# Eight of twenty weight subtractions move from GpSimd to VectorE

## The chip, the cores and the metric

The kernel runs on one core of a Trainium2 chip. The time is the device time of one execution in microseconds (us), and lower is better. TensorE multiplies matrices and accumulates in PSUM banks; VectorE, ScalarE and GpSimd do elementwise work; the queue of SyncE (SP) issues the DMAs between device memory and the on-chip SBUF. In the profile they are called PE (with PEld for its weight loads), DVE, ACT, POOL and SP. Each engine takes its own instructions strictly in the order in which they stand in its queue, and waits for the others by semaphores.

## The reference

One layer of a decoder, for 1024 tokens of width 1024, all in float32:

```python
h = rmsnorm(x, norm1_w)
proj = h @ w_in                       # one projection for both mixers
# mixer A: gated DeltaNet, 4 heads of 128; causal conv + silu on q, k, v; z is its gate
o_a = rmsnorm(gated_delta_rule(l2norm(q), l2norm(k), v, g, beta), gdn_norm_w) * silu(z)
# mixer B: dilated sliding-window attention, 8 heads of 64
o_b = dilated_attention(qb, kb, vb)
x = x + concat([o_a, o_b]) @ w_out
h = rmsnorm(x, norm2_w)
u = causal_dwconv(h @ w_up, ffn_conv_w)
x = x + (silu(u[..., :D_FF]) * u[..., D_FF:]) @ w_down
return rmsnorm(x, final_norm_w)
```

The delta rule works on chunks of tokens, and in each chunk a unit lower-triangular system is solved.

## The kernel before

**Products in three parts.** To keep float32 accuracy, each operand of a large product is split into a high part in TensorE's faster format (`whi`, `xhi`) and a low part (`wlo`, `xlo`), the difference between the operand and its high part. A product is then three products, high by high, high by low and low by high (`mm3`, line 200).

**The weights of the input projection.** `dense` (line 496) goes through 29 tiles of weights of 128 by 1024 numbers, in this order by index: 0 is the key tile of DeltaNet head 3; 1 to 8 are the values of the dilated attention; 9 to 16 are the query and value tiles of the four DeltaNet heads, one after the other; 17 to 24 are the query and key tiles of the dilated attention; 25 to 28 are the gate's tiles. The keys of heads 0 to 2 come earlier and are not in this list. While one tile is multiplied, the next is made: a DMA brings the raw weights (`wst`, two buffers), ScalarE copies them to `whi` (two buffers), and another engine subtracts: `wlo = wst - whi` (two buffers). Which engine subtracts is set by `spare` in `weight` (line 217): with it GpSimd, without it VectorE (through `split`, line 208).

**What runs beside it.** TensorE is given its work in an order that a planner (`Weave`) makes from estimated times: the dense products, and between them short products of the chunks. In the stretch that matters here VectorE has four kinds of work in one queue: it scales each half of a finished tile out of its PSUM banks (`xr`, two banks of the tag hf in turn); it adds up the causal convolution (`qT`, `vT`, three instructions each); it scales the attention scores of DeltaNet (`at`, four instructions for each of two banks of the tag atr); and it solves the triangular systems of all heads at once (`forward_sub`: 31 pairs of a product `tmp<-mt,xi` and a subtraction `xi<-xi,tmp`, each of which needs the one before). GpSimd has, beside the subtractions, only small work there: it clears buffers and takes a power for the norm of the queries (`rq<-ssq,mhalf`), which VectorE needs for `gq`.

**Order around the change.** The banks of the tag atr are shared: TensorE turns `qT` into token order there, makes the scores of head after head there, and turns `vT` there. The turns of `vT` (`ps<-ident,vT`, line 197, four to a bank) can start when VectorE has read the scores of the bank before (`at`). When the solve is done, its result goes to device memory and comes back by 24 strided loads on SP's queue (`x<-xdram`, `um<-xtdram`), for small merging products on TensorE. Inside VectorE's queue the order is set when the program is built, by a scheduler that goes by priorities and its own simulated times; what the code writes first need not stand first.

## Time and profile before

| | us |
|---|---|
| median of 3 runs (lowest, highest) | 1204.37 (1203.77, 1204.42) |
| the profiled execution | 1206.67 |
| its span, first to last instruction | 1204.6 |
| TensorE busy | 1191.6 |
| VectorE busy | 916.1 |
| ScalarE busy | 575.3 |
| GpSimd busy | 108.2 |
| subtractions on GpSimd | 20, of 2.38 each (median) |
| subtractions on VectorE, 128x1024 | 16, of 1.22 each (median of its 21) |

The program's instructions stand under the line of the helper that recorded them, so L142 is nearly all of VectorE, ScalarE and GpSimd, and L193 and L197 are TensorE; groups are told apart by their tiles, written out<-in. "Idle before" is the time in which the engine did nothing before an instruction, and what follows the arrow is what ended it. All times in the trace count from the start of the span.

### The profile page before, as it was taken

To read this page: it belongs to the slowest core of one execution; us is meant where nothing else is said; L and a number is where in the kernel's file an instruction comes from. 1 tells how busy PE (TensorE), PEld (TensorE's weight loads), DVE (VectorE), ACT (ScalarE), POOL (GpSimd) and SP (SyncE) were. 2 spreads that over 40 slices of the span, in tenths; PEclk is the share of its full clock that TensorE was granted. 3 is DMA by queue.
4 is the path that set the end of the run, shared out by engine and by line. 5 is a ranking of instruction groups with operands and counts; after the bars stand their busy time and mean duration, and the time that the engine had idled before them with its cause. 6 is when DMAs were issued, how large, how long until landed. Compare 5 with 4: busy or idle time off the path is not lost.

```text
span 1204.6 us, 18326 instructions
## 1 busy us (share of the span) xinstructions
PE 1191.6 (99%) x7068; PEld 987.0 (82%) x7068; DVE 916.1 (76%) x1442; ACT 575.3 (48%) x1126; POOL 108.2 (9%) x98
## 2 busy tenths in 40 slices
PE   9999999999999999999999999999999999999997
PEld 7888778889877778888888888888888888888886
DVE  7583985656365466767989989889898889999875
ACT  7375335456355443655545544444454454444441
POOL 0313232213422110000000000000000000000000
PEclk9999999999999999999999999999999999999998
DMA  7434233435624304444213122131322298547513
GB/s 235 107 93 121 103 109 119 149 115 164 222 94 128 95 36 120 169 140 140 84 56 106 58 100 91 67 105 53 105 73 85 94 370 305 180 162 226 165 54 140
DMA packets 85798, 154.80 MB, mean 129 GB/s; under 512 B 21168, under 2 KB 36304, under 8 KB 85712
## 3 DMA queue, kind: packets, MB, share of 16 engines
q1 hardware_dynamic: 85136, 153.12, 39.1%
q8 instruction: 55, 0.90, 0.3%
q10 hardware_dynamic: 576, 0.52, 0.1%
q14 instruction: 31, 0.25, 0.1%
HBM read 117.68 MB, written 35.93 MB: 128 GB/s over the span
## 4 chain that ended last, share of the span: by engine, by line
PE 93%; DVE 4%; ACT 1%; issue 1%; DMA 1%; SPq 0%; POOLq 0%; POOL 0%; DVEq 0%; ACTq 0%
PE ps L193 43%; PE pa L193 20%; PE dw L193 17%; PE pc L193 10%; PE ps L197 3%; DVE tmp L142 1%; DVE xi L142 1%; PE warm L193 1%; ACT sm L144 0%; DMA mt<-mdram 0%; DVE xr L142 0%; DVE qT L142 0%; DVE vT L142 0%; DMA mdram<-um 0%; DVE x1h L142 0%
## 5 line engine op out<-in xcount | busy, mean ns | idle before, releaser
L193 PE MATMUL dw<-pr 128*128 128x512 f32 (+1 forms) x984 | 211.3, 376 | 0.0
L193 PEld LDWEIGHTS dw<-pr 128*128 128x128 f32 x984 | 176.7, 188 | 33.6
L193 PE MATMUL ps<-xhi,whi 128*128 128x512 f32 x384 | 157.9, 411 | 0.5 <-DVE xr L142 0.5
L193 PE MATMUL ps<-xhi,wlo 128*128 128x512 f32 x384 | 150.5, 392 | 0.0
L193 PE MATMUL ps<-xlo,whi 128*128 128x512 f32 x384 | 150.3, 392 | 0.0
L193 PE MATMUL pa<-T,pair 128*128 128x512 f32 x528 | 127.0, 389 | 0.0
L193 PEld LDWEIGHTS pa<-T,pair 128*128 128x128 f32 x528 | 99.0, 188 | 20.6
L193 PEld LDWEIGHTS ps<-xhi,whi 128*128 128x128 f32 x384 | 72.7, 189 | 19.1 <-issue 5.6
L193 PEld LDWEIGHTS ps<-xhi,wlo 128*128 128x128 f32 x384 | 72.4, 188 | 15.8
L193 PEld LDWEIGHTS ps<-xlo,whi 128*128 128x128 f32 x384 | 72.7, 189 | 12.3
L142 ACT ACTIVATE u<-pa 128x512 f32<-128x512 f32 x44 | 26.3, 598 | 107.3 <-PE pa L193 107.3
L142 ACT ACTIVATE whi<-wst 128x1024 fp32r<-128x1024 f32 (+2 forms) x41 | 41.8, 1019 | 72.1 <-PE ps L193 40.3
L142 DVE SCALAR_TENSOR_TENSOR y<-xu,fcw,y 128x1023 f32<-128x1023 f32 (+1 forms) x44 | 56.4, 1281 | 22.1 <-ACT y L142 22.0
L142 POOL TENSOR_TENSOR rs<-rs,mhalf 128x2 f32<-128x2 f32 (+2 forms) x4 | 4.5, 1116 | 738.7 <-DVE rs L144 738.7
L193 PE MATMUL pc<-T,S 128*128 128x512 f32 x264 | 63.4, 389 | 0.0
L193 PE MATMUL pc<-B,pair 128*128 128x512 f32 x264 | 63.4, 389 | 0.0
L193 PE MATMUL pa<-B,A 128*128 128x512 f32 x264 | 63.4, 389 | 0.0
L193 PE MATMUL pa<-T,S 128*128 128x512 f32 x264 | 63.4, 389 | 0.0
L142 DVE TENSOR_TENSOR wst<-wst 128x512 f32<-128x512 f32 x88 | 60.5, 687 | 0.9
L193 PE MATMUL ps<-B,pair 128*128 128x512 f32 x252 | 60.5, 389 | 0.0
L144 ACT ACTIVATE sm<-sm,mx 128x128 f32<-128x128 f32 (+7 forms) x64 | 35.4, 555 | 47.9 <-DVE mx L144 47.9
L142 POOL TENSOR_TENSOR wlo<-wst,whi 128x1024 fp32r<-128x1024 f32 x20 | 47.9, 2393 | 115.6 <-ACT whi L142 113.7
(246 smaller groups left out, 2417.5 us busy)
## 6 DMA issues: line engine op xcount, KB each, us to landing
wst<-in_wu SPq DMA_DIRECT2D x44, 512.0 KB, 3.7
wd<-in_wd SPq DMA_DIRECT2D x44, 512.0 KB, 4.5
upark<-y SPq DMA_DIRECT2D x22, 512.0 KB, 3.7
wst<-in_wi SPq DMA_DIRECT2D x21, 512.0 KB, 3.7
r<-upark SPq DMA_DIRECT2D x11, 512.0 KB, 7.8
r<-upark SPq DMA_DIRECT2D x22, 256.0 KB, 6.8
wa<-in_wd SPq DMA_DIRECT2D x22, 256.0 KB, 3.1
wst<-in_wv SPq DMA_DIRECT2D x8, 512.0 KB, 3.7
```

What stands on the lines that cost most here:

```text
L142: return getattr(eng, op)(*a, **kw)
L144: return getattr(eng, op)(*a, **kw)
L193: tc.stamp_issue_order_token(nc.tensor.matmul(dst, lhs, rhs, start=start, stop=stop, **kw).ins, TOKEN)
L197: tc.stamp_issue_order_token(nc.tensor.transpose(dst, src, ident if idt is None else idt).ins, TOKEN)
```

## The change

The condition `spare` turns from index 9 on to index 17 on. GpSimd keeps the subtractions of 17 to 28, twelve in all: the query and key tiles of the dilated attention and the gate's four. Those of 9 to 16, the query and value tiles of DeltaNet, go to VectorE.

```diff
@@ -517,7 +517,7 @@
             w = nxt.pop()
             i = place[0] = place[0] + 1
             if i < len(srcs):
-                nxt.append(weight(None, st=raw.pop(), spare=i >= 9))
+                nxt.append(weight(None, st=raw.pop(), spare=i >= 17))
             if i + 1 < len(srcs):
                 raw.append(raw_weight(srcs[i + 1]))
             return w
```

The order of instructions on TensorE and on ScalarE is the same in both programs. Three places of the others follow.

GpSimd loses the eight subtractions; this is the piece of the difference (x_1647 and x_1661 are the buffers that the solve's result comes back to).

```order
 L142 TENSOR_TENSOR nk<-ssk,phalf 128x8 x4
-L142 TENSOR_TENSOR wlo<-wst,whi 128x1024
 L142 MEMSET xi 128x1024
 L142 AFFINE_SELECT xi<-xi 128x1024
-L142 TENSOR_TENSOR wlo<-wst,whi 128x1024 x3
-L142 TENSOR_TENSOR rq<-ssq,mhalf 128x8
-L142 TENSOR_TENSOR wlo<-wst,whi 128x1024 x2
+L142 TENSOR_TENSOR rq<-ssq,mhalf 128x8 x2
 L142 MEMSET x_1647 128x1024
 L142 MEMSET x_1661 128x1024
```

Two of the eight stand ahead of the clearing of `xi` and of the solve, and the others among the solve's steps.

VectorE in the first part of the solve, where the first convolution stands, before:

```order
L142 TENSOR_TENSOR tmp<-mt,xi 128x231
L142 TENSOR_TENSOR xr<-ps,rstdB 128x512
L142 TENSOR_TENSOR xi<-xi,tmp 128x21x11
L142 TENSOR_TENSOR tmp<-mt,xi 128x240
L142 TENSOR_TENSOR xi<-xi,tmp 128x20x12
L142 SCALAR_TENSOR_TENSOR qT<-xr,gcw,qT 128x1023
L142 TENSOR_TENSOR tmp<-mt,xi 128x247
L142 SCALAR_TENSOR_TENSOR qT<-xr,gcw,qT 128x1022
L142 TENSOR_TENSOR xi<-xi,tmp 128x19x13
L142 SCALAR_TENSOR_TENSOR qT<-xr,gcw,qT 128x1021
L142 TENSOR_TENSOR xr<-ps,rstdB 128x512
```

The same place now:

```order
L142 TENSOR_TENSOR xr<-ps,rstdB 128x512
L142 TENSOR_TENSOR tmp<-mt,xi 128x231
L142 TENSOR_TENSOR wlo<-wst,whi 128x1024
L142 TENSOR_TENSOR xi<-xi,tmp 128x21x11
L142 SCALAR_TENSOR_TENSOR qT<-xr,gcw,qT 128x1023
L142 TENSOR_TENSOR tmp<-mt,xi 128x240
L142 SCALAR_TENSOR_TENSOR qT<-xr,gcw,qT 128x1022
L142 TENSOR_TENSOR xi<-xi,tmp 128x20x12
L142 TENSOR_TENSOR xr<-ps,rstdB 128x512
L142 SCALAR_TENSOR_TENSOR qT<-xr,gcw,qT 128x1021
```

One subtraction has come in, the next tile's `xr` stands ahead of the third convolution step, and two steps of the solve (247) have gone behind it.

VectorE at the scores, before:

```order
L142 TENSOR_TENSOR tmp<-mt,xi 128x240
L142 TENSOR_TENSOR xr<-ps,rstdB 128x512
L142 TENSOR_TENSOR xi<-xi,tmp 128x12x20
L142 SCALAR_TENSOR_TENSOR at<-ps,bp,dec 128x128 x4
L142 SCALAR_TENSOR_TENSOR gq<-ngam,rq 128x8
L142 TENSOR_TENSOR tmp<-mt,xi 128x231
L142 TENSOR_TENSOR xi<-xi,tmp 128x11x21
L142 TENSOR_TENSOR tmp<-mt,xi 128x220
L142 SCALAR_TENSOR_TENSOR at<-ps,bp,dec 128x128 x4
```

The same place now:

```order
L142 TENSOR_TENSOR tmp<-mt,xi 128x252
L142 TENSOR_TENSOR xr<-ps,rstdB 128x512
L142 SCALAR_TENSOR_TENSOR at<-ps,bp,dec 128x128 x4
L142 SCALAR_TENSOR_TENSOR gq<-ngam,rq 128x8
L142 TENSOR_TENSOR xi<-xi,tmp 128x14x18
L142 TENSOR_TENSOR tmp<-mt,xi 128x247
L142 SCALAR_TENSOR_TENSOR at<-ps,bp,dec 128x128
L142 TENSOR_TENSOR xi<-xi,tmp 128x13x19
L142 SCALAR_TENSOR_TENSOR at<-ps,bp,dec 128x128 x3
```

The scores stand earlier among the solve's steps: the solve has got to 252 instead of to the subtraction with 12x20 when the first bank is read, which is five steps fewer.

## The prediction

> **What bounds the kernel now.** I read the page first, then TensorE's waits, then the chain of waits around them, then the timelines of the engines there.

> ```profile
> PE 1191.6 (99%) x7068; PEld 987.0 (82%) x7068; DVE 916.1 (76%) x1442; ACT 575.3 (48%) x1126; POOL 108.2 (9%) x98
> PE 93%; DVE 4%; ACT 1%; issue 1%; DMA 1%; SPq 0%; POOLq 0%; POOL 0%; DVEq 0%; ACTq 0%
> ```

> TensorE is busy for 99% of the span and holds 93% of the chain that ended last; VectorE holds 4% of it. TensorE's products are the same and in the same order after the change, so the time moves only by what TensorE waits, or by its clock. The subtractions concerned lie between 110 and 196 us. All of TensorE's waits there that the view of waits names (window 120 to 160) are these three, and none is listed between 160 and 245:

> ```profile
> PE ps L197 <- DVE at L142: 1.6, 1, 1.6
> PE ps L193 <- DVE xr L142: 0.5, 1, 0.5
> PE ps L197 <- DVE gq L142: 0.3, 1, 0.3
> ```

> All three are for VectorE. The chain of waits (window 130 to 160; start, length, what) shows how far back that goes:

> ```profile
> 127.95 2.48 DVE tmp L142
> ...
> 136.15 1.27 DVE qT L142
> ...
> 139.76 0.44 DVE tmp L142
> ...
> 141.70 1.97 DVE xi L142
> ...
> 152.40 1.05 DVE at L142 x4
> 153.49 1.10 PE ps L197 x4
> ```

> For 25 us the chain runs through VectorE's queue, but for one ScalarE step, and it holds two pieces that are far too long: a step of the solve of 2.48 and one of 1.97, beside one of 0.44 between them. The timeline of GpSimd and VectorE (start, length) tells why:

> ```profile
> 127.64 2.53 POOL L142 TENSOR_TENSOR wlo<-wst,whi 128x1024 fp32r<-128x1024 f32 x1 [7.73 <-ACT whi L142]
> 127.95 2.46 DVE L142 TENSOR_TENSOR tmp<-mt,xi 128x220 f32<-128x220 f32 x1
> 130.45 0.39 DVE L142 TENSOR_TENSOR xi<-xi,tmp 128x220 f32<-128x220 f32 x1
> 140.88 2.50 POOL L142 TENSOR_TENSOR wlo<-wst,whi 128x1024 fp32r<-128x1024 f32 x1 [10.71 <-ACT whi L142]
> 141.02 0.68 DVE L142 TENSOR_TENSOR xr<-ps,rstdB 128x512 f32<-128x512 f32 x1
> 141.62 2.04 DVE L142 TENSOR_TENSOR xi<-xi,tmp 128x255 f32<-128x255 f32 x1
> 144.15 0.42 DVE L142 TENSOR_TENSOR xi<-xi,tmp 128x252 f32<-128x252 f32 x1
> ```

> While GpSimd subtracts, a VectorE instruction with two inputs in SBUF does not finish until GpSimd is done; `xr`, with an input in PSUM, runs on. The first held step loses 2.46 - 0.39 = 2.07, the second 2.04 - 0.42 = 1.62. So GpSimd, 9% busy, stands on the chain through VectorE.

> What it costs on TensorE, from its timeline at the three places:

> ```profile
> 137.28 0.39 PE L193 MATMUL ps<-xhi,wlo 128*128 128x512 f32 x1
> 138.17 0.47 PE L193 MATMUL ps<-xhi,whi 128*128 128x512 f32 x1 [0.50 <-DVE xr L142]
> ...
> 139.17 0.39 PE L193 MATMUL ps<-xlo,whi 128*128 128x512 f32 x1
> 139.40 0.39 PE L193 MATMUL ps<-xhi,wlo 128*128 128x512 f32 x1
> 139.91 0.55 PE L197 MATMUL ps<-ident,qT 128*128 128x128 f32 x3
> ```

> ```profile
> 150.62 0.39 PE L193 MATMUL ps<-xhi,wlo 128*128 128x512 f32 x1
> 151.30 0.63 PE L197 MATMUL ps<-ident,vT 128*128 128x128 f32 x4 [0.29 <-DVE gq L142]
> 153.49 1.10 PE L197 MATMUL ps<-ident,vT 128*128 128x128 f32 x4 [1.56 <-DVE at L142]
> 154.24 0.78 PE L193 MATMUL ps<-xhi,whi 128*128 128x512 f32 x1
> ```

> A product takes 0.23 from start to start (139.17 to 139.40). So 137.28 to 138.17 loses 0.66, 139.40 to 139.91 loses 0.28 (the turns wait for ScalarE's `qT`, whose input VectorE finished at 136.15 + 1.27), and 150.62 to 151.30 loses 0.45. Where TensorE stood idle, the loss is the idle time and 0.16, by which a product's row (0.39) otherwise overlaps the next: so the 1.56 ahead of 153.49 are 1.72 lost. Together 3.11. Then the clock, in two windows:

> ```profile
> 150.00:153.54 3.54, 1.69 (x10) 0.98 (x8) 3.47 (x14) 0.05 (x2) 0.71 (x1) 1.00 0.00 0
> 153.54:156.96 3.42, 3.42 (x11) 2.84 (x12) 2.34 (x7) 2.38 (x9) 0.00 (x0) 0.50 0.38 153
> ```

> The columns are window, length, then PE, PEld, DVE, ACT and POOL busy, clock, and DMA. After a stretch with TensorE 1.69 busy of 3.54, it gets half its clock for 3.42 us: 1.71 lost. In all 4.82 us hang on VectorE being late here.

> [...]

> **The change part by part.** Row by row for the subtraction itself (min/median/max in ns, first and last start):

> ```profile
> L142 DVE TENSOR_TENSOR wlo<-wst,whi x21: 558/1224/1227, 4.3 to 540.0; 128x1024 fp32r<-128x1024 f32 x16, 128x768 fp32r<-128x768 f32 x3, 128x384 fp32r<-128x384 f32 x2
> L142 POOL TENSOR_TENSOR wlo<-wst,whi x20: 2352/2382/2532, 110.6 to 452.2; 128x1024 fp32r<-128x1024 f32 x20
> ```

> *GpSimd* loses 8 x 2.38 = 19.1 us. It waited for `whi` before each, so this in itself is worth nothing. *VectorE* gains 8 x 1.22 = 9.8 us. The first two stand ahead of the solve, where VectorE waits anyway:

> ```profile
> 121.56 0.19 DVE L142 TENSOR_TENSOR tmp<-mt,xi 128x31 f32<-128x31 f32 x1 [10.05 <-DMA mt<-mdram]
> ```

> They cost nothing; without that idle time it would be 2.4. The third and fourth stand ahead of the scores: +2.44. Against that the two held steps give back 2.07 + 1.62 = 3.69, and the new order puts five solve steps behind the scores, about 0.41 each as in the rows above: 2.04. VectorE reaches `gq` 3.69 + 2.04 - 2.44 = 3.29 earlier. From `gq` to the end of the second bank it now has two solve steps, one score, one solve step, three scores, 0.12 more than before. It ended those scores at 152.40 + 1.05 = 153.45, and now ends them at 153.45 - 3.29 + 0.12 = 150.28. TensorE, freed of the four stalls, would want that bank at 153.49 - 3.11 = 150.38. So the stall goes with 0.1 to spare: the lead and the need are about equal, and whatever else makes VectorE late comes back on TensorE.

> What else could: VectorE takes over GpSimd's wait for `whi`, and behind it everything in its queue stands.

> ```profile
> 126.50 1.06 ACT L142 ACTIVATE whi<-wst 128x1024 fp32r<-128x1024 f32 x1 [9.06 <-PE ps L193]
> 137.50 1.28 ACT L142 ACT_TABLE_LOAD   x1 [4.44 <-DVE qT L142]
> 139.76 1.04 ACT L142 ACTIVATE whi<-wst 128x1024 fp32r<-128x1024 f32 x1
> 147.78 2.93 POOL L142 TENSOR_TENSOR rq<-ssq,mhalf 128x8 f32<-128x8 f32 x1 [4.40 <-DVE ssq L142]
> ```

> The third `whi` is ready at 127.56, and VectorE gets to its subtraction at about 129.4: no wait. The fourth is ready at 140.80, behind a table load that itself waits for the third step of `qT`. That step comes about 1 earlier now (-2.07, +1.22, +0.6 for `xr`, -0.7 for the two steps gone behind), so `whi` comes at about 139.8, and VectorE gets there at 140.20 - 2.07 + 1.22 + 0.6 = 139.95, where 140.20 is the end of the solve step that stands before it (139.76 + 0.44). No wait then, or 0.9 if ScalarE does not come earlier. I take 0.4, between the ends, since both margins are thin. `rq` (2.93 while VectorE was busy) starts some 3 earlier with its input, and is ready before `gq`.

> The fifth subtraction, too, held a solve step:

> ```profile
> 158.11 2.43 DVE L142 TENSOR_TENSOR xi<-xi,tmp 128x156 f32<-128x156 f32 x1
> ```

> TensorE has no wait from 157 to 245, so what the last four give back is worth nothing, and their 4 x 1.22 = 4.9 in VectorE's queue cost nothing as long as they come back about as they are added. The solve ends later: in the new order the three convolution steps of the second value tile (1.27 each, by `qT`) and two `xr` (0.6 each) stand ahead of its last step, 5.0 in all, from which the lead of 3.3 is to be taken or not: 2 to 5 us. With it its 24 loads come later on SP, and one weight load now passes ahead of them instead of waiting behind.

> ```profile
> 167.19 0.33 SPq L142 DMA_DIRECT2D xdram<-xi  x1
> 174.42 1.98 SPq L142 DMA_DIRECT2D x<-xdram  x4
> 191.99 0.69 PE L193 MATMUL ps<-x,um 32*32 32x32 f32 x32
> ```

> The first merges need only the first loads, issued by 174.42 + 1.98 = 176.4 before. TensorE gets there 4.4 earlier and they come at most 5 later: 191.99 - 176.4 - 9.4 leaves 6.2, landing included. Hidden; without that cover each us late would be one lost.

> Sum: 0.66 + 0.28 + 0.45 + 1.72 + 1.71 - 0.4 = 4.4 us off. Against this execution's own 1206.67 that is 1202.3. The median of the runs shown is 2.3 below it, and 1204.37 - 4.4 = 1200.0. Ends: 4.8 off (1199.6) if VectorE is never late, 1.4 off if the wait at the scores stays.

> **The rivals.** *The half clock stays*, or the timed runs never had it (they lie 2.3 below the profiled one and within 0.65 of each other, so all have it or none): 4.4 - 1.7 = 2.7, so 1201.7. *The scores' bank still binds*: if VectorE is late by more than 1.72 against the sum, only the first three terms go, 1.4 off: 1203.0. For it speaks the 0.1 of margin, against it that everything ahead is counted from rows. *Slower, by waiting at the head of the queue*: VectorE stands for `whi` at the subtractions from the third on. A wait there may be the table load's 1.28. The subtractions are in the sum already; standing so at four of them, 4 x 1.28 = 5.1, eats the lead of 3.29 and leaves 1.8 more stall than before, 1206.2, and with a second fall of the clock of 1.71 1207.9. It decides the sign once the waits pass 3.29. Against it: `whi` was ready first at the third, and ScalarE is 48% busy. *It does not act*: the order shows the eight moved, so this is only that nothing comes of it: 1204.4.

> **How the numbers follow.** All gone: 0.50, 1200.0. Clock loss not in it: 0.22, 1201.7. Bank still binds: 0.16, 1203.0. No effect: 0.04. Slower: 0.08. About 0.2%, or 2.4 us, is what a measurement of this kernel can tell from no change, so faster is below 1201.96: 0.50 and most of the 0.22, 0.70. Same is 0.16 + 0.04 and the rest, 0.22; slower 0.08. The range goes from 1198.9 (4.8 off, and 0.65 for the spread of the runs) to 1203.3, where the bank's case ends; the likeliest alone has 1199.3 to 1201.2.

> **What would show it.** Right: no solve step above 0.45 between 120 and 155, `wlo` on VectorE twenty-nine times, no wait of TensorE for `at` above 0.5, no stretch of clock 0.50 near 150, and VectorE's first score there before 147.5. Wrong: VectorE idle ahead of `wlo` for `whi`, or TensorE's wait for `at` still there, or new waits for `x` or `um` at the merges.

## The result, and the profile after

The changed kernel takes 1202.16 us (median of 14 runs, 1200.98 to 1202.87), the kernel before beside it 1205.15 (median of 14, 1203.67 to 1208.6). The ratio is 0.9975, with a 95% interval of 0.9968 to 0.9981: 3.0 us faster. The profiled execution took 1202.47, its span 1200.5. The forecast was 1200.0 with a range to 1203.3, and 4.4 us off.

From the page of the changed kernel, the busy times and the shares of the chain that ended last:

```profile
PE 1189.1 (99%) x7068; PEld 985.9 (82%) x7068; DVE 916.3 (76%) x1450; ACT 574.9 (48%) x1126; POOL 87.6 (7%) x90
PE 95%; DVE 2%; ACT 1%; issue 1%; POOLq 0%; POOL 0%; DVEq 0%; ACTq 0%
```

VectorE has eight instructions more and is as busy as before (916.3 against 916.1): the eight subtractions add 9.8, and its `tmp`, `xi`, `qT` and `vT` rows, no longer held, are 9.3 shorter in sum. Its share of the chain falls from 4% to 2%. In the view of waits, TensorE has none at all between 105 and 250 us. VectorE's timeline at the places of the two held steps and at the scores:

```profile
128.93 0.39 DVE L142 TENSOR_TENSOR tmp<-mt,xi 128x220 f32<-128x220 f32 x1
130.56 1.22 DVE L142 TENSOR_TENSOR wlo<-wst,whi 128x1024 fp32r<-128x1024 f32 x1
140.37 1.22 DVE L142 TENSOR_TENSOR wlo<-wst,whi 128x1024 fp32r<-128x1024 f32 x1
144.63 0.43 DVE L142 TENSOR_TENSOR xi<-xi,tmp 128x255 f32<-128x255 f32 x1
147.09 1.13 DVE L142 SCALAR_TENSOR_TENSOR at<-ps,bp,dec 128x128 f32<-128x128 f32 x4
149.58 0.86 DVE L142 SCALAR_TENSOR_TENSOR at<-ps,bp,dec 128x128 f32<-128x128 f32 x3
```

The step of width 220 that took 2.46 takes 0.39, that of 255 takes 0.43 instead of 2.04, and neither subtraction has idle time ahead of it (there is no bracket). The second score bank is done at 149.58 + 0.86 = 150.44. TensorE there, and the same two windows as in the forecast:

```profile
139.87 1.03 PE L197 MATMUL ps<-ident,qT 128*128 128x128 f32 x8
150.75 1.04 PE L197 MATMUL ps<-ident,vT 128*128 128x128 f32 x8
165.27 1.03 PE L197 MATMUL ps<-ident,qT 128*128 128x128 f32 x8
```

```profile
150.00:153.54 3.54, 3.54 (x22) 2.99 (x21) 3.06 (x9) 2.15 (x9) 0.00 (x0) 1.00 0.37 148
153.54:156.96 3.42, 3.42 (x17) 2.83 (x16) 3.39 (x6) 2.01 (x3) 0.00 (x0) 1.00 0.06 10
```

The eight turns of `vT` go through in one piece instead of four and four with 1.56 us between them, and the clock stays at 1.00 (the last but two of the columns). What was gained between two fixed points of TensorE's work shows best: the last product of the values ahead of the stretch, and the turns of the next head's `qT` behind it. In TensorE's timeline of the kernel before:

```profile
114.92 0.39 PE L193 MATMUL ps<-whi,xhi 128*128 128x512 f32 x1
...
169.22 1.04 PE L197 MATMUL ps<-ident,qT 128*128 128x128 f32 x8
```

and of the changed one the first point:

```profile
116.07 0.39 PE L193 MATMUL ps<-whi,xhi 128*128 128x512 f32 x1
```

From point to point it took 54.30 us and now takes 49.20 (165.27 - 116.07): 5.1 off, where the forecast's terms for this stretch add up to 4.82. The first point itself came 1.15 later in this execution, mostly behind a wait of 0.9 for ScalarE that the unchanged kernel has in other executions too (below). That leaves about the 4.1 between the two spans.

### The profile page after: what moved, and what is told of

It is laid out like the page before. It is cut to its first block, busy times and chain, and to the rows that moved or that the text cites. A ratio compares the mean times of both kernels' runs of the same rounds, so it can differ in the third digit from the quotient of the medians.

```text
span 1200.5 us, 18328 instructions
## 1 busy us (share of the span) xinstructions
PE 1189.1 (99%) x7068; PEld 985.9 (82%) x7068; DVE 916.3 (76%) x1450; ACT 574.9 (48%) x1126; POOL 87.6 (7%) x90
## 4 chain that ended last, share of the span: by engine, by line
PE 95%; DVE 2%; ACT 1%; issue 1%; POOLq 0%; POOL 0%; DVEq 0%; ACTq 0%
PE ps L193 45%; PE pa L193 20%; PE dw L193 17%; PE pc L193 10%; PE ps L197 3%; DVE kT L142 1%; PE warm L193 1%; ACT sm L144 0%; DVE xr L142 0%; DVE x1h L142 0%; PE pd L193 0%; DVE zz L142 0%; ACT dec L142 0%; ACT xr L142 0%; ACT whi L142 0%
## 5 line engine op out<-in xcount | busy, mean ns | idle before, releaser
L193 PE MATMUL dw<-pr 128*128 128x512 f32 (+1 forms) x984 | 211.3, 376 | 0.0
L193 PEld LDWEIGHTS dw<-pr 128*128 128x128 f32 x984 | 176.7, 188 | 33.6
L193 PE MATMUL ps<-xhi,whi 128*128 128x512 f32 x384 | 157.2, 409 | 0.0
L193 PE MATMUL ps<-xhi,wlo 128*128 128x512 f32 x384 | 150.0, 391 | 0.0
L193 PE MATMUL ps<-xlo,whi 128*128 128x512 f32 x384 | 149.8, 390 | 0.0
L193 PE MATMUL pa<-T,pair 128*128 128x512 f32 x528 | 127.1, 389 | 0.0
L193 PEld LDWEIGHTS pa<-T,pair 128*128 128x128 f32 x528 | 98.9, 188 | 20.6
L193 PEld LDWEIGHTS ps<-xhi,whi 128*128 128x128 f32 x384 | 72.2, 188 | 17.9 <-issue 4.7
L193 PEld LDWEIGHTS ps<-xhi,wlo 128*128 128x128 f32 x384 | 72.1, 188 | 15.7
L193 PEld LDWEIGHTS ps<-xlo,whi 128*128 128x128 f32 x384 | 72.3, 188 | 12.3
L142 ACT ACTIVATE u<-pa 128x512 f32<-128x512 f32 x44 | 26.3, 598 | 107.3 <-PE pa L193 107.3
L142 ACT ACTIVATE whi<-wst 128x1024 fp32r<-128x1024 f32 (+2 forms) x41 | 41.8, 1020 | 71.9 <-PE ps L193 56.0
L142 DVE SCALAR_TENSOR_TENSOR y<-xu,fcw,y 128x1023 f32<-128x1023 f32 (+1 forms) x44 | 56.4, 1281 | 22.1 <-ACT y L142 22.0
L193 PE MATMUL pa<-B,A 128*128 128x512 f32 x264 | 63.4, 389 | 0.0
L193 PE MATMUL pc<-T,S 128*128 128x512 f32 x264 | 63.4, 389 | 0.0
L193 PE MATMUL pa<-T,S 128*128 128x512 f32 x264 | 63.4, 389 | 0.0
L193 PE MATMUL pc<-B,pair 128*128 128x512 f32 x264 | 63.4, 389 | 0.0
L142 DVE TENSOR_TENSOR wst<-wst 128x512 f32<-128x512 f32 x88 | 60.6, 688 | 0.9
L193 PE MATMUL ps<-B,pair 128*128 128x512 f32 x252 | 60.5, 389 | 0.0
L142 ACT ACTIVATE pr<-r 128x1024 fp32r<-128x1024 f32 (+1 forms) x44 | 36.4, 839 | 47.5 <-PE dw L193 30.1
L142 POOL TENSOR_TENSOR rs<-rs,mhalf 128x2 f32<-128x2 f32 (+2 forms) x4 | 4.5, 1116 | 738.7 <-DVE rs L144 738.7
```

The source lines that it names most:

```text
L142: return getattr(eng, op)(*a, **kw)
L193: tc.stamp_issue_order_token(nc.tensor.matmul(dst, lhs, rhs, start=start, stop=stop, **kw).ins, TOKEN)
```

## The experiments

Each was timed beside the kernel before on one chip. The diffs are against the kernel before; where only a plus line stands, it takes the place of the line with `spare=i >= 9`.

**The same kernel again, and the two halves of the cause.** My theory was that GpSimd's subtraction holds VectorE. The rival was that the change acts by the new order of VectorE's queue. Three kernels tell them apart: the kernel before without any edit (`again`); its own order without the two holds (`clear`); and the changed kernel's order with the two holds put back (`hold`).

> The kernel before, unchanged, run once more: it is to show whether the half clock near 153 us and TensorE's waits of 0.5, 0.3 and 1.6 us for VectorE come in every execution. If the fall of the clock belongs to the stall, the profile has clock 0.50 for about 3.4 us behind the 1.6 us wait, and the mean clock of the timed runs is 0.996 as in the first profile. If the fall depends on where the stall happens to lie against a window of the clock's own, some executions have a mean clock of 0.997 to 0.998, and the profile may have no fall; then the executions differ by up to 1.7 us among themselves. Time: the same as before within 0.1%.

> The kernel before, in which GpSimd at indices 11 and 12 clears the buffer of the low part instead of subtracting (the low parts of these two tiles are left out, so two products use a zero). The order of every engine is that of the kernel before; only the two instructions that held VectorE no longer read SBUF. Theory (GpSimd's subtraction holds VectorE, and that alone makes VectorE late): VectorE is 2.07 + 1.62 = 3.7 us earlier at the scores, all three waits of TensorE near 137 to 153 go, and the time falls by 3 to 4.8 us, as much as the change gave. Rival (the new order of VectorE's queue gave it, the solve's steps behind the scores): the waits stay, and the time is that of the kernel before within 1 us.

```diff
-        if spare:
+        if spare == 2:
+            ac.activation(hi, st, AF.Copy)
+            po_.memset(lo.bitcast(F32), 0.0)
+        elif spare:
...
-                nxt.append(weight(None, st=raw.pop(), spare=i >= 9))
+                nxt.append(weight(None, st=raw.pop(), spare=2 if i in (11, 12) else i >= 9))
```

> The changed kernel, in which GpSimd, beside VectorE's own subtraction, subtracts the tiles of indices 11 and 12 once more into a buffer that nothing reads, in two halves. The order of VectorE, ScalarE and TensorE is that of the changed kernel. Theory (the hold): VectorE's solve steps there are held again, 1 to 3.7 us in all, the lead of 3.3 us at the scores is eaten, TensorE waits for the scores again, and the time is 1 to 5 us above the changed kernel, near the kernel before. Rival (the new order): the time stays that of the changed kernel, 3 us below the kernel before, since the order is the same.

```diff
+        dead = cp.tile([P, 512], F32, name="dead")
...
-                nxt.append(weight(None, st=raw.pop(), spare=i >= 9))
+                st = raw.pop()
+                nxt.append(weight(None, st=st, spare=i >= 17))
+                if i in (11, 12):
+                    for h in range(2):
+                        po_.tensor_tensor(dead, st[:, half(h)], nxt[-1][0][:, half(h)].bitcast(F32), op=OP.subtract)
```

The last column is the stretch between the two points of TensorE's work from above, in the profiled execution.

| kernel | order of VectorE | holds | median us | ratio to before (95%) | stretch us |
|---|---|---|---|---|---|
| `again` | before | yes | 1205.21 | 0.9998 (0.9989 to 1.0007) | 52.13 |
| `clear` | before | no | 1202.12 | 0.9969 (0.9957 to 0.9981) | 49.20 |
| `hold` | after | yes | 1205.92 | 0.9998 (0.9989 to 1.0007) | 53.13 |
| the changed kernel | after | no | 1202.16 | 0.9975 (0.9968 to 0.9981) | 49.20 |

The times go by the holds. Without them the old order is as fast as the new one, and with them the new order gains nothing. `hold` differs from the changed kernel by the added subtractions alone; it is not quite the kernel before with another order, since VectorE has its own two subtractions there as well. `clear`, timeline of GpSimd (first row) and VectorE:

```profile
127.18 0.96 POOL L142 MEMSET wlo<- 128x1024 f32 x1 [6.79 <-PE ps L193]
127.27 0.38 DVE L142 TENSOR_TENSOR xi<-xi,tmp 128x207 f32<-128x207 f32 x1
127.68 0.39 DVE L142 TENSOR_TENSOR tmp<-mt,xi 128x220 f32<-128x220 f32 x1
```

GpSimd writes the same tile while VectorE's steps run beside it at their usual 0.38 and 0.39, so that GpSimd is at work is not enough to hold them. `hold`, the same two engines:

```profile
127.21 2.77 POOL L142 TENSOR_TENSOR dead<-wst,whi 128x512 f32<-128x512 f32 x2 [13.78 <-ACT whi L142]
127.49 1.34 DVE L142 TENSOR_TENSOR xi<-xi,tmp 128x207 f32<-128x207 f32 x1
128.87 1.35 DVE L142 TENSOR_TENSOR tmp<-mt,xi 128x220 f32<-128x220 f32 x1
141.28 1.22 DVE L142 TENSOR_TENSOR wlo<-wst,whi 128x1024 fp32r<-128x1024 f32 x1
141.33 3.75 POOL L142 TENSOR_TENSOR dead<-wst,whi 128x512 f32<-128x512 f32 x2 [11.35 <-issue]
142.41 1.52 DVE L142 TENSOR_TENSOR xi<-xi,tmp 128x256 f32<-128x256 f32 x1
143.85 2.31 DVE L142 SCALAR_TENSOR_TENSOR vT<-xr,gcw,vT 128x1023 f32<-128x1023 f32 x1
```

Cut in two, the subtraction holds two steps for about 1 us each (1.34 and 1.35 against 0.38 and 0.39) instead of one for 2. Nobody needs its result, so what VectorE waits for is the instruction's run itself. The convolution step `vT`, which reads `xr` and `vT`, is held as well, 2.31 against 1.28. And it goes both ways: where VectorE's own subtraction had begun 0.05 earlier (141.28), GpSimd's two halves took 3.75 instead of 2.77. So these rows show VectorE's steps held by a subtraction on GpSimd (1.34 and 1.35) and not by a clearing (0.38 and 0.39), and GpSimd held beside a subtraction on VectorE (3.75).

`hold` and `again`, TensorE's waits between 105 and 250 us:

```profile
PE ps L197 <- ACT qT L142: 1.8, 1, 1.8
PE ps L197 <- DVE at L142: 1.5, 1, 1.5
```

```profile
PE ps L197 <- DVE at L142: 1.6, 1, 1.6
PE ps L197 <- DVE gq L142: 0.3, 1, 0.3
```

`again` has two of the three waits of the kernel before (1.6 and 0.3); the 0.5 for `xr` is missing, since TensorE came to that place later, behind the wait for ScalarE. In its windows the half clock is missing too:

```profile
150.12:153.53 3.41, 1.61 (x9) 0.90 (x7) 3.34 (x14) 0.00 (x1) 0.67 (x1) 1.00 0.00 0
153.54:156.96 3.42, 3.39 (x17) 2.89 (x18) 3.21 (x9) 3.29 (x10) 0.14 (x1) 1.00 0.38 153
```

The second window is at clock 1.00, where the profiled execution of the kernel before had 0.50. So the fall of the clock follows the stall in some executions and not in others.

**Which of the eight.** Two kernels split the eight subtractions: `two` moves only indices 11 and 12 to VectorE, `sixkeep` only the other six.

> Only the subtractions of indices 11 and 12 go to VectorE; the other eighteen stay on GpSimd. Theory (only these two are on the chain): nearly all of the gain. VectorE's lead at the scores is 3.69 for the two holds, less 2.44 for the two subtractions, and 1.2 for three solve steps that now stand behind the scores: 2.5, and two steps fewer than three stand between the two banks, 0.4: so a wait of 0 to 0.5 us is left and the time is 2.5 to 4.5 us below the kernel before. Rival (all eight matter, or the earlier subtractions): clearly less than the change's 3.0, under 1.5.

```diff
+                nxt.append(weight(None, st=raw.pop(), spare=i >= 9 and i not in (11, 12)))
```

> The change without its two that count: six of the eight go to VectorE, and the subtractions of indices 11 and 12 stay on GpSimd. Theory (only these two are on the chain): the two holds of about 2 us stay, VectorE is at most 0.8 us earlier at the scores through two solve steps that moved behind them, TensorE's wait there stays above 0.8 us, and the time is that of the kernel before within about 1 us. Rival (all eight matter alike): three quarters of the change's gain, 2.2 us.

```diff
+                nxt.append(weight(None, st=raw.pop(), spare=i >= 17 or i in (11, 12)))
```

`two` takes 1202.58 (0.998, 0.9969 to 0.999) and has most of the gain. Its stretch is 49.95, with 0.5 of waiting for `qT` left. Two of its eight runs are near 1205, the profiled one (1205.01) among them; that one has a wait of 1.1 for ScalarE's `sq` near 168 us, which no other trace shows at that place. `sixkeep` takes 1206.04 (1.0003, 0.9994 to 1.0012) and has none. Its waits of TensorE, and its windows:

```profile
PE ps L197 <- DVE at L142: 1.6, 1, 1.6
PE ps L193 <- DVE xr L142: 0.4, 1, 0.4
PE ps L197 <- DVE gq L142: 0.3, 1, 0.3
```

```profile
151.49:154.90 3.41, 1.54 (x11) 1.26 (x11) 3.27 (x12) 0.83 (x4) 0.00 (x0) 1.00 0.03 13
154.90:158.31 3.41, 3.41 (x10) 2.62 (x9) 2.92 (x9) 3.00 (x8) 0.00 (x0) 0.50 0.35 141
```

These are the three waits of the kernel before, and here the half clock came too, for 3.41 us again; the stretch is 54.1, near the 54.3 of the kernel before.

Then one index at a time, to see whether the delays add up in VectorE's queue or the nearest one decides:

> Only index 11, whose subtraction held a step of the solve by 2.07, goes to VectorE. If delays add up in VectorE's queue, its second score bank ends 2.07 - 1.22 + 0.41 (one solve step fewer ahead of the scores) = 1.26 us earlier, TensorE's waits for xr and ScalarE's qT go, its wait for at stays at 1 us or more, and the time is 1.3 us off. If only the hold nearest to the scores counts, nothing is off. If either one of the two is enough to set VectorE free, 3 us are off.

```diff
+                nxt.append(weight(None, st=raw.pop(), spare=i >= 9 and i != 11))
```

> Only index 12, whose subtraction held a step by 1.62, goes to VectorE. If delays add up, the second bank ends 1.62 - 1.22 + 0.41 + 0.40 (one solve step fewer ahead of gq, and one fewer behind it) = 1.21 us earlier: 1.2 us off, with TensorE's wait for xr at 138 still there. If only the hold nearest to the scores counts, 3 us are off; if only the earlier one, nothing.

```diff
+                nxt.append(weight(None, st=raw.pop(), spare=i >= 9 and i != 12))
```

`one_a` takes 1203.77 (0.9983, 0.9974 to 0.9991), `one_b` 1203.64 (0.9984, 0.9975 to 0.9993): each has about half of the gain. Part of it is the half clock, which shows in none of their 23 runs (how it is told is said below). Against the 14 runs of the kernel before without it, median 1205.1 in this comparison, they are 1.3 and 1.5 faster, and `twin`, the changed kernel in the same comparison, is 3.2 faster: the two add up to nearly the whole, and each is near the 1.3 and 1.2 expected. Their stretches, of single executions, are 51.89 and 50.70 against the 52.13 of `again`, which is less alike; `one_a` is the one of the three without the wait for `sq`. What is left of the wait for `at` stands in the waits of each:

```profile
PE ps L197 <- DVE at L142: 1.5, 1, 1.5
PE ps L197 <- ACT qT L142: 0.4, 1, 0.4
PE ps L197 <- DVE gq L142: 0.2, 1, 0.2
```

```profile
PE ps L193 <- ACT sq L144: 0.8, 1, 0.8
PE ps L197 <- DVE at L142: 0.6, 1, 0.6
```

The first is `one_a`, the second `one_b` (window 60 to 250; the wait for `sq` lies ahead of the stretch). Held by the other subtraction, VectorE is late again, by less. Both theories of a single decisive hold fall. My expectation for `one_a` had TensorE's wait for `qT` gone, and 0.4 of it stayed; that for `one_b` had the wait for `xr` staying, and it was gone. `one_b` has the wait for `sq`, as `again` has, so there, too, TensorE comes later to that place.

**How far the change should go.** Three kernels move the others of the twenty: `att` takes the gate's four to VectorE as well, `gate` the eight of the dilated attention instead, `none` all twelve.

> As the change, and the gate's four subtractions go to VectorE as well; GpSimd keeps the eight of the dilated attention. The kernel before shows two holds of some 1.3 us there, on the gate's own VectorE work (427.95 and 453.16), and TensorE's only waits near are 0.2 us for ScalarE. Theory (holds matter only where VectorE is on the chain): the same as the changed kernel within 0.5 us. Rival (every hold costs): 1 to 2.5 us below the changed kernel.

```diff
+                nxt.append(weight(None, st=raw.pop(), spare=17 <= i < 25))
```

> As the change, and the eight subtractions of the dilated attention's tiles go to VectorE as well; GpSimd keeps the gate's four. In the kernel before VectorE's work beside those eight reads PSUM, and GpSimd's 2.4 us hold none of it. Theory (a hold is what costs, and there are none here): nothing to gain, and 1.22 us more in VectorE's queue each, where the delta rule's chain waits for VectorE: 0 to 3 us above the changed kernel. Rival (VectorE's subtraction is faster, so the weights come earlier and TensorE waits less): below the changed kernel.

```diff
+                nxt.append(weight(None, st=raw.pop(), spare=i >= 25))
```

> All twenty subtractions on VectorE. By the theory of the holds: as the run in which only the gate's four are left to GpSimd, within 0.5 us, so 0 to 3 us above the changed kernel. Rival (GpSimd's part in the subtractions is a loss everywhere): the fastest of all.

```diff
+                nxt.append(weight(None, st=raw.pop(), spare=False))
```

`att` takes 1201.71 (0.9965, 0.9952 to 0.9977), `gate` 1203.78 (0.9983, 0.9974 to 0.9992), `none` 1204.68 (0.9987, 0.9978 to 0.9996). The eight of the attention are better left on GpSimd: `none` differs from `att` by these eight alone and loses 3.0 us, and `gate` differs from the changed kernel by them alone and is 1.6 slower, though in another comparison. In `att`, `gate`, `none` and the changed kernel the stretch of above is 49.2, so the loss lies behind it. My expectation for `none` had it within 0.5 of `gate`, and it is 0.9 above. That for `gate` said that GpSimd holds none of VectorE's work beside the eight; in the kernel before it does hold two convolution steps there (2.44 at 215.94 and 2.18 at 234.51), and no wait of TensorE comes of it. All of TensorE's waits that are named in `none` between 245 and 470:

```profile
PE ps L193 <- ACT w L144: 0.5, 1, 0.5
PE ps L193 <- DVE ct L144: 0.4, 1, 0.4
PE ps L193 <- DVE pb L144: 0.3, 2, 0.2
PE ps L193 <- DVE vtok L144: 0.3, 1, 0.3
```

The changed kernel lists there the first two and 0.2 for `sm`. The waits for VectorE's `pb` and `vtok`, 0.6, are new. The rest shows in TensorE's score products of the attention, `kT,qT` 64x256 and 64x128, between 222 and 390: the same 68 and 12 take 11.2 and 2.4 us in `none` where they take 9.7 and 1.5 in `att`. That is 2.4 more, and with the 0.6 it makes the 3.0. What these products wait for, in pieces too short to be idle time, was not tested.

Since `att` had come out below the changed kernel, though in another comparison, both were run once more side by side:

> The changed kernel once more, beside the kernel before on the same chip, as the measure for the other three. Expected: 3.0 us off again, between 2.3 and 3.9, no wait of TensorE between 105 and 250 us, and no stretch of half clock.

> GpSimd keeps only the subtractions of 17 to 24; the gate's four go to VectorE together with 9 to 16. It was 4.1 us under the kernel before when it was run first, the changed kernel 3.0, in another run of the chip. If the gate's subtractions on GpSimd hold VectorE where TensorE waits for it, it is 1 us under the changed kernel here too. If not, the two agree within 0.5 us, and the difference was that of the two comparisons.

`twin` takes 1201.93 (0.9964, 0.9952 to 0.9976), `att_two` 1201.82 (0.9966, 0.9954 to 0.9978). They are the same; no version beat the change.

## Why the prediction came out as it did

**The mechanism, right.** GpSimd's subtraction held VectorE, and the two held steps were what made TensorE wait. `clear` and `hold` show it from both sides, in the time and in the stretch, and `one_a`, `one_b` and `two` that the two delays add up.

**The terms of the sum.** The forecast had 3.11 us of waits, 1.71 of half clock and 0.4 kept back, 4.4 off.

- *The half clock, 1.71: the step that failed.* Its size was right, but I took it to be in every execution, by the argument that the three timed runs lie within 0.65 us of each other, so all have it or none. In the last three comparisons the kernel before ran 75 times with its mean granted clock on record. 33 runs show 0.996, with a median of 1206.8, and 42 show 0.997 or 0.998, with a median of 1205.1; of the 11 runs of `again`, the same program, 5 show 0.996. The profiled executions with the half clock (before, `sixkeep`) have 0.996 and that of `again`, without it, 0.998. So the fall came in about 4 of 10 executions and cost about 1.7 in those. The count is a lower bound: every trace also ends with 6.2 to 9.7 us at clock 0.50 on its clock record (8.9 in the kernel before, 8.0 in the changed one), so the traces without the fall have means of 0.9969 to 0.9983, and the fall takes 0.0014 off. All 19 runs of the changed kernel, 14 and the 5 of `twin`, show 0.997 or 0.998. The three runs from which the 1.71 was taken off, 1203.77 to 1204.42, lie below every one of the 33 (1205.64 at least), so most likely none of them had it to lose.
- *The waits less the reserve, 3.11 - 0.4 = 2.7.* Against executions of the kernel before without the fall, the changed kernel is 1205.1 - 1202.16 = 2.9 faster; against those with it 1206.8 - 1202.16 = 4.6, where the forecast said 4.4. The first rival ("the timed runs never had it", 2.7 off) and the likeliest case were thus each right for a part of the executions, and the median of all falls between them, at 3.0. It should have been forecast as 2.7 plus 1.71 times the share of executions with the fall. The stretch says the same of single executions: 52.13 - 49.20 = 2.9 without the fall, and 5.10 with it, of which 5.10 - 1.71 = 3.4 are waits where the sum had 3.11. The 0.66 for `xr` among them is not in every execution either (`again` loses only 0.24 at that place, 137.79 to 138.26 less the usual 0.23).
- *The reserve of 0.4 for `whi`: not needed in this stretch.* The third and fourth subtractions had no idle time ahead of them. Behind it VectorE does stand for `whi`, once for 0.64 (at 179.94), where nothing waits for it.
- *The level.* The kernel before came out at 1205.15 over 14 runs, 0.8 above the three runs from which 4.4 was taken off. That moves the forecast time, not the gain. Of the 2.2 by which 1202.16 lies above 1200.0, 0.8 is the level and 1.4 the gain; the nearest single forecast was the first rival's 1201.7. My line for faster, below 1201.96, was missed by 0.2 for the same reason, since it was drawn from the three runs.

**The margin at the second score bank.** The forecast had the bank done at 150.28 and wanted at 150.38. In the changed kernel it was done at 150.44 and wanted at 151.19 (the fifth of the eight turns from 150.75), 0.75 to spare instead of 0.1. TensorE had come 1.15 later to the stretch, but VectorE's solve, too, began 0.97 later (122.53 against 121.56), so that is not the reason. From there to the end of the bank VectorE needs 27.91 instead of 31.89, 3.98 less, where the sum had 3.29 - 0.12 = 3.17. What was sized too small is mainly the solve's steps, taken at 0.41 each. Where one follows the other directly, as in the kernel before, it is 0.46 from start to start (139.76 to 140.22), and where another instruction stands between, as in the new order, 0.33 (140.04 to 140.37). The bank did not bind in the other executions without holds either: `clear` came to these turns at 150.08 and `gate` at 149.17, and neither waits for `at`. So the second rival, 1203.0, did not come about.

**The slower rival** needed waits of VectorE for `whi` beyond 3.29 us. There were none ahead of the scores, so it had nothing to stand on.

**The solve.** The forecast had it end 2 to 5 us later, hidden at the merges. The copy of its result in the changed kernel:

```profile
171.05 1.12 DVE L142 COPY mt<-xi 128x1024 f32<-128x1024 f32 x1
```

Before, the same copy began at 167.20, so it comes 3.85 later (0.97 of it because the solve began later), and no wait of TensorE appears at the merges.

**The marks that I gave.** Every one of the right ones is there but for a detail: the solve's steps are at most 0.43 between 120 and 155, `wlo` is on VectorE 29 times, TensorE does not wait for `at`, the clock does not fall near 150, and the first score there begins at 147.09, against 147.5 at the latest. The detail is that one mark, the missing half clock, proves less than I thought: `again` lacks it as well, with the stall still there.

## What to carry to other kernels

An engine that is nearly idle and on no chain can still be the cause of one: look in the bottleneck's feeder for instructions several times as long as their neighbours of the same shape, and at what ran beside them. Of twenty subtractions on GpSimd only the two that overlapped the steps ahead of TensorE's wait cost anything; moving eight more of them to VectorE took back 1.6 to 3 us. And a loss seen in one profile has to be weighed by how often it occurs: here the granted clock of every run told in how many.

## What the hardware showed that I had not expected

| kernel | window | TensorE busy, us | clock behind |
|---|---|---|---|
| before | 150.13 to 153.54 | 1.56 | 0.50 |
| `sixkeep` | 151.47 to 154.89 | 1.55 | 0.50 |
| `hold`, ahead of the turns of `qT` | 137.14 to 140.55 | 1.60 | 1.00 |
| `one_a` | 149.37 to 152.79 | 1.81 | 1.00 |
| `hold`, at the scores | 150.80 to 154.21 | 1.91 | 1.00 |
| `again` | 149.47 to 152.88 | 2.26 | 1.00 |
| `again` | 152.88 to 156.29 | 2.72 | 1.00 |

In the kernel before and in `sixkeep` the stall lies whole in one window. `again` has practically the same stall (1.61 busy from 150.12 to 153.53), but a boundary of its grid cuts it in two at 152.88, and the halves have 2.26 and 2.72. In these rows the two windows that cost the clock have TensorE busy for 1.56 and 1.55 of 3.41 us, the five that did not for 1.60 and more. The limit is not settled: 1.56 cost it and 1.60 did not, in one window each, the windows ahead of the falls at the end have 1.87 (before, 1194.61 to 1198.02) and 1.61 (the changed kernel, 1191.29 to 1194.70), and the ends of TensorE's instructions are modelled in the profile. Nor is the share of the executions: in the kernel before a window with at most 1.58 busy, between the 1.56 and the 1.60, could begin anywhere from 150.06 to 151.02, which for a grid placed at random gives an estimate of 0.96 / 3.413 = 0.28, and the count was 33 of 75. `one_a`, whose stretch never falls below 1.75, had 0.996 in none of its 12 runs. `hold`, with two stalls, shows 0.995 in 2 of its 11, and whether both cost it there is not on record.

In the two windows of the table that cost the clock no single gap of TensorE is above 1.6 us: the longest are the waits for `at`, 1.56 in the kernel before and 1.57 in `sixkeep`.

The second surprise is a wait that comes and goes. In ten of the fourteen profiled executions, that of the changed kernel and of `again` among them, TensorE waits 0.7 to 0.9 us for ScalarE's `sq` between 60 and 105 us, ahead of all that was changed; in those of the kernel before, `hold`, `gate` and `one_a` it does not. It shifts every later time of a trace, which is mostly why the spans differ by 4.1 and the stretch itself by 5.1, and it can take the place of a later wait, as that for `xr` in `again`. Why it comes was not tested.
